# Three instead of two gate/up chunks by seven block products in three feed-forward layers, with plain chunks split between the halves of the features

## The chip, the cores and the metric

The kernel runs on one core of one Trainium2 chip. The metric is device time in microseconds (us) of one execution; the median of three runs stands for the kernel.

## The reference

A two-layer model on 256 tokens of 1024 features. Each layer is a half-weighted feed-forward block, a mixer (two kinds of attention) and another half-weighted feed-forward block; a norm closes the model. The change touches the feed-forward blocks alone:

```
D_MODEL, SEQ, DEPTH, D_FF = 1024, 256, 2, 2816

def swiglu(x, w_gate, w_up, w_down):
    return (jax.nn.silu(x @ w_gate) * (x @ w_up)) @ w_down

    for l in range(DEPTH):
        x = x + 0.5 * swiglu(rms_norm(x, ffa_norm[l]), ffa_w_gate[l], ffa_w_up[l], ffa_w_down[l])
        x = x + hybrid_mixer(rms_norm(x, mix_norm[l]), w_in[l], ...)
        x = x + 0.5 * swiglu(rms_norm(x, ffb_norm[l]), ffb_w_gate[l], ffb_w_up[l], ffb_w_down[l])
    return rms_norm(x, final_norm)
```

So there are four feed-forward blocks, called layers 0 to 3 here. All arrays are fp32.

## The kernel before

**Arithmetic.** Every fp32 matrix is split into a high and a low part (ScalarE copies the high part, L302 `whi`; VectorE subtracts it, L281 `wlo`), and every product is three matmuls of 128 x 512: high by high, low by high, high by low (`prod3`, L321 to L323).

**Weights.** The unit is a block of 512 rows by 512 columns (1 MB). `loader` brings blocks from HBM into five `raw` slots through SyncE's queue (L247, L238). `splitter` takes them in the order of the plan and splits each in two halves of 128 x 1024 into a pool of six `whi`/`wlo` pairs, so that three units are split ahead at most. TensorE frees a pair when it has used it.

**Gate and up.** The 2816 features are five chunks of 512 (0 to 4) and a rest `h5` of 256. A *plain* chunk c is `gc` and `uc`: the gate and the up weights, each two units (`kh`, the halves of the rows), each unit 24 matmuls. The other form takes a chunk's 2 x 2 block product (token halves by feature halves against gate and up) in *seven* block products instead of eight, with sums of blocks on both sides; each is one unit of 12 matmuls. The plan writes them as two digits: `53` is product 5 of chunk 3. The sums of activation blocks are made once for a layer (L515 to L530). The sums of weight blocks are made by DMA: an *add* of the next block onto the raw slot whose contents have just been split (`adder`, GpSimd's queue, L261, `accum_op=OP.add`). So products 1, 5, 6, 4 are a chain in one raw slot (three adds, the last with a gate block), 3 and 7 a chain in a second (one add), and 2 is a plain load. A slot in a chain is free again only after the last split of the chain. What leaves PSUM of such a chunk goes through `rest`, seven VectorE operations (L629 to L654) and two turns (transposes by TensorE, L549, and `hlo`, L556); a plain chunk has two VectorE operations (L574) and two turns.

**Order.** The program is written by a recorder with a clock of its own (class `Flow`); each engine then executes its instructions strictly in the written order, and waits for semaphores. The plan sets the order of the products on TensorE and of the splits:

```
PLANS = ("g0 u0 g2 11 u2 51 21 31 13 61 71 g4 41 53 23 33 u4 63 73 h5 43".split(),) + (
    "g0 u0 11 g2 51 21 31 u2 61 71 13 g4 41 53 23 33 u4 63 73 h5 43".split(),) * 3
```

The first plan is layer 0's, the second that of layers 1, 2 and 3. After gate and up comes the down product (11 units of 24 matmuls).

Of the kernel before, what the change touches and what calls it, by code (L numbers as in the profile page):

```python
# [41 lines left out]
ARRIVE_X = [3.5, 5.9, 8.1, 10.3]  # L42
HOP = 0.3
PLANS = ("g0 u0 g2 11 u2 51 21 31 13 61 71 g4 41 53 23 33 u4 63 73 h5 43".split(),) + (
    "g0 u0 11 g2 51 21 31 u2 61 71 13 g4 41 53 23 33 u4 63 73 h5 43".split(),) * 3
AC = 0.1
DV = 0.06

# [84 lines left out]
def hybrid_kernel(ctx, tc, x_in, ffa_norm, ffa_w_gate, ffa_w_up, ffa_w_down, mix_norm, w_in,  # L133
# [85 lines left out]
    def order(src, a, b, loads=1, **k):  # L219
        return Unit(Raw(src, a, b, loads), fine=loads > 1, **k)  # L220
# [95 lines left out]
    def cols(w, c0, n, kh):  # L316
        return w[kh * 512:(kh + 1) * 512, c0:c0 + n].rearrange("(k p) n -> p k n", p=128)
# [126 lines left out]
    def ffn_units(wg, wu, wd, plan, first):  # L444

        us = {}
        chain = {}

        def block(c, m, kh):
            return cols((wg, wu)[m], c * 512, 512, kh)

        def step(key, c, p, m, kh, end):

            src = block(c, m, kh)
            if key not in chain:
                chain[key] = (Raw(src, 4, 512), None)
                r = chain[key][0]
            else:  # L460
                r = Sum(chain[key][0], src, chain[key][1])
            us[p, c] = Unit(r, done=end)
            chain[key] = (chain[key][0], us[p, c])

        for z in plan:
            kind, c = z[0], int(z[1:])
            if kind in "gu":
                m = "gu".index(kind)
                for kh in range(2):
                    us[z, kh] = order(block(c, m, kh), 4, 512, loads=4 if first and z == plan[0] else 1)  # L470
            elif kind == "h":
                for kh in range(2):
                    us[z, kh] = order([cols(wg, 2560, 256, kh), cols(wu, 2560, 256, kh)], 4, 512)
            elif kind in "1564":
                step(("x", c), c, kind, *{"1": (0, 0), "5": (1, 0), "6": (1, 1), "4": (0, 1)}[kind], kind == "4")
            elif kind in "37":
                step(("y", c), c, kind, *{"3": (1, 1), "7": (1, 0)}[kind], z == [q for q in plan if q[0] in "37" and q[1:] == z[1:]][-1])
            else:
                step(("z", c), c, kind, 0, 1, True)
        for j in range(11):  # L480
            src = wd[j * 256:(j + 1) * 256].rearrange("(i p) n -> p i n", i=2)
            us["d", j] = order(src, 2, 1024)
        return us

    def ffn(us, nm, nxt, plan, last=False):
        hs = (big.tile([128, 22, 256], F32R, name="hhi", tag="hhi"),
              big.tile([128, 22, 256], F32R, name="hlo", tag="hlo"))
        rs = [nm.rs[:, t:t + 1] for t in range(T)]
        neg = small.tile([128, T], F32, name="neg", tag="neg", bufs=2)
        ev = {(c, t): Event() for c in range(6) for t in range(T)}  # L490
        sgs, forms, evs = {}, {}, {}
        inner = [i for i, z in enumerate(plan) if z[0] in "1234567"]

        def event(*k):
# [1135 lines left out]
```

## Time and profile before

| what | before |
|---|---|
| median of 3 runs | 1004.54 us (1003.06 to 1004.55) |
| the profiled execution's own time | 1003.62 us |
| its span, first to last instruction | 1001.8 us |
| TensorE / VectorE / ScalarE busy | 99% / 73% / 61% |
| gate/up stage of layers 1, 2, 3 (span's clock) | 321.7 to 441.2, 502.8 to 622.4, 813.4 to 933.0 us |

The span leaves out 1.8 us of the profiled execution's time. A stage is counted from the first matmul with the layer's normed input to the first with the gated features (`hhi`).

### The profile page before, as it was taken

How to read it: one execution, taken by the hardware profiler on the slowest of the kernel's cores; microseconds unless marked ns; L12 is line 12 of the kernel's file. 1: busy time of each engine (PE TensorE's matmuls, PEld its weight loads, DVE VectorE, ACT ScalarE, POOL GpSimd, SP SyncE). 2: the span in 40 equal slices, each digit the busy share in tenths (PEclk: the TensorE clock that was granted, in tenths of full speed). 3: DMA queues.
4: the chain of work that ended last, by engine and by line, in shares of the span. 5: the costliest groups of instructions: out<-in, count | busy, mean ns of one | idle time of the engine just before them, and what ended most of it. 6: DMA issues, size and time to landing. Idle time of an engine off the chain costs nothing.

```text
span 1001.8 us, 14198 instructions
## 1 busy us (share of the span) xinstructions
PE 988.3 (99%) x5270; PEld 825.7 (82%) x5270; DVE 735.8 (73%) x1369; ACT 608.0 (61%) x1055; POOL 53.5 (5%) x61
## 2 busy tenths in 40 slices
PE   8999999999999999999999999999999999999996
PEld 7888788898987888888888888888988878888885
DVE  6988764688887978784498768447878789788544
ACT  7667453558786676653367565336687766675531
POOL 1021000100000011100001110001000001110000
PEclk9999999999999999999999999999999999999999
DMA  9899965363743799965558998553655248999611
GB/s 334 273 198 303 290 241 183 106 193 119 260 145 103 208 248 278 274 251 200 179 151 229 300 262 274 196 166 116 211 188 191 86 130 226 281 264 305 237 48 42
DMA packets 100981, 207.62 MB, mean 207 GB/s; under 512 B 3784, under 2 KB 23376, under 8 KB 100912
## 3 DMA queue, kind: packets, MB, share of 16 engines
q1 hardware_dynamic: 83072, 171.65, 49.2%
q0 software_dynamic: 17536, 34.54, 19.3%
q8 instruction: 41, 0.67, 0.3%
q10 hardware_dynamic: 304, 0.53, 0.1%
q14 instruction: 28, 0.23, 0.1%
HBM read 205.66 MB, written 1.05 MB: 206 GB/s over the span
## 4 chain that ended last, share of the span: by engine, by line
PE 86%; DMA 4%; DVE 2%; ACT 1%; issue 1%; DVEq 0%; POOL 0%; ACTq 0%
PE acc L321 17%; PE acc L322 17%; PE acc L323 17%; PE sb L323 6%; PE sb L321 6%; PE sb L322 6%; PE acc L338 2%; DMA raw<-in_ffa_w_up_dram 2%; PE acc L339 2%; PE acc L340 2%; PE acc L1079 2%; PE tb L1059 2%; DMA raw<-in_ffa_w_gate_dram 2%; PE tb L549 2%; PE tb L407 1%; DVE wlo L281 1%
## 5 line engine op out<-in xcount | busy, mean ns | idle before, releaser
L281 DVE TENSOR_TENSOR wlo<-raw,whi 128x1024 fp32r<-128x1024 f32 (+2 forms) x404 | 450.2, 1136 | 166.7 <-ACT whi L302 166.3
L302 ACT ACTIVATE whi<-raw 128x1024 fp32r<-128x1024 f32 (+2 forms) x404 | 388.7, 990 | 239.7 <-PE acc L323 103.8
L321 PE MATMUL acc<-whi,hhi 128*128 128x512 f32 x352 | 138.4, 393 | 0.0
L323 PE MATMUL acc<-whi,hlo 128*128 128x512 f32 x352 | 137.2, 390 | 0.0
L322 PE MATMUL acc<-wlo,hhi 128*128 128x512 f32 x352 | 137.0, 389 | 0.0
L321 PE MATMUL acc<-whi,xhi 128*128 128x512 f32 (+1 forms) x336 | 131.9, 393 | 0.0
L322 PE MATMUL acc<-wlo,xhi 128*128 128x512 f32 (+1 forms) x336 | 128.1, 381 | 0.0
L323 PE MATMUL acc<-whi,xlo 128*128 128x512 f32 (+1 forms) x336 | 127.9, 381 | 0.0
L321 PE MATMUL sb<-whi,xhi 128*128 128x512 f32 x304 | 119.3, 392 | 0.0
L322 PE MATMUL sb<-wlo,xhi 128*128 128x512 f32 x304 | 118.4, 390 | 0.6 <-DVE wlo L281 0.6
L323 PE MATMUL sb<-whi,xlo 128*128 128x512 f32 x304 | 118.5, 390 | 0.0
L323 PEld LDWEIGHTS acc<-whi,hlo 128*128 128x128 f32 x352 | 66.1, 188 | 14.0
L322 PEld LDWEIGHTS acc<-wlo,hhi 128*128 128x128 f32 x352 | 66.1, 188 | 13.3
L321 PEld LDWEIGHTS acc<-whi,hhi 128*128 128x128 f32 x352 | 66.1, 188 | 13.4
L323 PEld LDWEIGHTS acc<-whi,xlo 128*128 128x128 f32 x336 | 63.1, 188 | 12.1
L321 PEld LDWEIGHTS acc<-whi,xhi 128*128 128x128 f32 x336 | 63.4, 189 | 11.2 <-issue 0.7
L322 PEld LDWEIGHTS acc<-wlo,xhi 128*128 128x128 f32 x336 | 63.2, 188 | 10.7 <-DVE wlo L281 0.2
L322 PEld LDWEIGHTS sb<-wlo,xhi 128*128 128x128 f32 x304 | 57.1, 188 | 12.6 <-DVE wlo L281 1.0
L323 PEld LDWEIGHTS sb<-whi,xlo 128*128 128x128 f32 x304 | 57.1, 188 | 12.0
L321 PEld LDWEIGHTS sb<-whi,xhi 128*128 128x128 f32 x304 | 57.1, 188 | 11.5
L338 PE MATMUL acc<-xhi,whi 128*128 128x256 f32 x192 | 56.5, 294 | 0.0
L340 PE MATMUL acc<-xhi,wlo 128*128 128x256 f32 x192 | 54.2, 282 | 0.0
(221 smaller groups left out, 1426.6 us busy)
## 6 DMA issues: line engine op xcount, KB each, us to landing
raw<-in_ffa_w_down_dram SPq DMA_DIRECT2D x22, 1024.0 KB, 5.0
raw<-in_ffb_w_down_dram SPq DMA_DIRECT2D x22, 1024.0 KB, 5.1
raw<-in_w_in_dram SPq DMA_DIRECT2D x20, 1024.0 KB, 5.1
raw<-in_ffb_w_gate_dram SPq DMA_DIRECT2D x20, 1024.0 KB, 5.2
raw<-in_ffa_w_gate_dram SPq DMA_DIRECT2D x18, 1024.0 KB, 7.4
raw<-in_ffa_w_up_dram SPq DMA_DIRECT2D x16, 1024.0 KB, 7.5
raw<-in_ffb_w_up_dram SPq DMA_DIRECT2D x16, 1024.0 KB, 6.4
raw<-in_ffa_w_up_dram POOLq DMA_DIRECT2D x12, 1024.0 KB, 9.3
```

Of the source, the lines that this page charges most:

```text
L281: nc.vector.tensor_tensor(view(u, lo, i, True), source(u, i), view(u, hi.bitcast(F32), i, True), OP.subtract)
L302: nc.scalar.activation(view(u, u.halves[-1][0], i, True), source(u, i), AF.Copy)
L321: nc.tensor.matmul(ps, xh, wh, start=first, stop=False, skip_group_check=True)
L322: nc.tensor.matmul(ps, xh, wl, start=False, stop=False, skip_group_check=True)
L323: nc.tensor.matmul(ps, xl, wh, start=False, stop=last, skip_group_check=True)
L338: nc.tensor.matmul(ps, wh, xs[0][:, k], start=first and j == 0, stop=False, skip_group_check=True)
L339: nc.tensor.matmul(ps, wh, xs[1][:, k], start=False, stop=False, skip_group_check=True)
L340: nc.tensor.matmul(ps, wl, xs[0][:, k], start=False, stop=last, skip_group_check=True)
L407: nc.tensor.transpose(ps[:, i * n + (t - ts[0]) * 128:i * n + (t - ts[0] + 1) * 128], x[:, t, k * 128:(k + 1) * 128], ident)
L549: nc.tensor.transpose(ps[:, j * 128:(j + 1) * 128], h[:, j * 128:(j + 1) * 128], ident)
L1059: nc.tensor.transpose(ps[:, j * 128:(j + 1) * 128], pp[:, i * n + s_ * 128:i * n + (s_ + 1) * 128], ident)
L1079: nc.tensor.matmul(grp.o[u * 64:(u + 1) * 64, h // 2 * 128:(h // 2 + 1) * 128], val(s_), pT[:, j * 128:(j + 1) * 128], start=u not in grp. ...
```

## The change

Layer 0 keeps its plan. In layers 1 to 3 chunk 2 too goes by seven products, chunk 4 stays plain and moves to the front, and of `u4` and `h5` the two units (`a`, `b`) may stand at different places of the plan; their PSUM sums wait in `parts` between the two.

```
-    "g0 u0 11 g2 51 21 31 u2 61 71 13 g4 41 53 23 33 u4 63 73 h5 43".split(),) * 3
+    "g0 u0 11 g4 51 21 12 31 22 61 u4a 52 u4b 13 32 71 41 62 23 53 72 h5a 33 42 63 h5b 73 43".split(),) * 3
...
-            kind, c = z[0], int(z[1:])
+            kind, c = z[0], int(z[1])
...
-                for kh in range(2):
-                    us[z, kh] = order(block(c, m, kh), 4, 512, loads=4 if first and z == plan[0] else 1)
+                for kh in rows_of(z):
+                    us[z[:2], kh] = order(block(c, m, kh), 4, 512, loads=4 if first and z == plan[0] else 1)
...
+    def rows_of(z):
+
+        return {"": (0, 1), "a": (0,), "b": (1,)}[z[2:]]
...
         def plain(z, tag, first):
-            c, then = int(z[1:]), {"g": gate, "u": up, "h": both}[z[0]]
-            ps = {}
-            for kh in range(2):
-                u = us[z, kh]
+            c, then = int(z[1]), {"g": gate, "u": up, "h": both}[z[0]]
+            ps = parts.setdefault(z[:2], {})
+            for kh in rows_of(z):
+                u = us[z[:2], kh]
```

Lines below L486 stand four lower in the changed kernel (L574 becomes L578, L549 becomes L553).

**VectorE, the long run.** Of before, layer 1, the splits of `41 53 23 33` (raw_3201 is chunk 1's chain, raw_3630 and raw_3862 are chunk 3's, raw_3770 is `23`), which are followed by the plain `u4`:

```order
L281 TENSOR_TENSOR wlo_3877<-raw_3201,whi_3876 128x1024
L281 TENSOR_TENSOR wlo_3892<-raw_3201,whi_3891 128x1024
L556 TENSOR_TENSOR hlo_3315<-tb_3885,hhi_3314 128x4x128
L281 TENSOR_TENSOR wlo_3905<-raw_3630,whi_3904 128x1024
L281 TENSOR_TENSOR wlo_3916<-raw_3630,whi_3915 128x1024
L281 TENSOR_TENSOR wlo_3934<-raw_3770,whi_3933 128x1024
L281 TENSOR_TENSOR wlo_3953<-raw_3770,whi_3952 128x1024
L649 TENSOR_TENSOR p_3563<-acc_3821,p_3563 128x512
L281 TENSOR_TENSOR wlo_3968<-raw_3862,whi_3967 128x1024
L281 TENSOR_TENSOR wlo_3980<-raw_3862,whi_3979 128x1024
L654 SCALAR_TENSOR_TENSOR p_3666<-p_3666,neg_3316,p_3563 128x512
```

Of the change, layer 1, from the end of `u4b` on: `32` (raw_3814), `71` (raw_3515), `41` (raw_3201), in which the two L578 take `u4`'s results out of PSUM.

```order
L578 SCALAR_TENSOR_TENSOR sg_3639<-sb_3780,rs_3234,sg_3639 128x512
L281 TENSOR_TENSOR wlo_3859<-raw_3814,whi_3858 128x1024
L578 SCALAR_TENSOR_TENSOR sg_3648<-sb_3790,rs_3234,sg_3648 128x512
L281 TENSOR_TENSOR wlo_3870<-raw_3814,whi_3869 128x1024
L560 TENSOR_TENSOR hlo_3315<-tb_3880,hhi_3314 128x4x128
L281 TENSOR_TENSOR wlo_3887<-raw_3515,whi_3886 128x1024
L560 TENSOR_TENSOR hlo_3315<-tb_3896,hhi_3314 128x4x128
L281 TENSOR_TENSOR wlo_3904<-raw_3515,whi_3903 128x1024
L281 TENSOR_TENSOR wlo_3922<-raw_3201,whi_3921 128x1024
L281 TENSOR_TENSOR wlo_3938<-raw_3201,whi_3937 128x1024
L638 TENSOR_TENSOR p_3666<-acc_3927,p_3666 128x512
L643 TENSOR_TENSOR z_3951<-acc_3644,p_3563 128x512
```

Before, four units in a row (with three other operations in the rows shown) are followed by a plain chunk; now `13 32 71 41 62 23 53 72` are eight in a row, and what three chunks and `u4` leave in PSUM stands between them.

**VectorE, the second part of that run.** Of before, behind the run, `u4` (raw_3898, raw_3921), `63` (raw_3630) and `73` (raw_3862):

```order
L281 TENSOR_TENSOR wlo_3997<-raw_3898,whi_3996 128x1024
L281 TENSOR_TENSOR wlo_4010<-raw_3898,whi_4009 128x1024
L556 TENSOR_TENSOR hlo_3315<-tb_4015,hhi_3314 128x4x128
L281 TENSOR_TENSOR wlo_4027<-raw_3921,whi_4026 128x1024
L281 TENSOR_TENSOR wlo_4040<-raw_3921,whi_4039 128x1024
L281 TENSOR_TENSOR wlo_4057<-raw_3630,whi_4056 128x1024
L281 TENSOR_TENSOR wlo_4068<-raw_3630,whi_4067 128x1024
L281 TENSOR_TENSOR wlo_4083<-raw_3862,whi_4082 128x1024
L281 TENSOR_TENSOR wlo_4094<-raw_3862,whi_4093 128x1024
```

Of the change: from the first split of `23` (raw_3934) over `53` (raw_3768) to the second of `72` (raw_3814). Three rows not shown (two splits of `62` and one L648) stand between the fence above and this one.

```order
L281 TENSOR_TENSOR wlo_3972<-raw_3934,whi_3971 128x1024
L653 TENSOR_TENSOR p_3563<-acc_3927,p_3563 128x512
L281 TENSOR_TENSOR wlo_3984<-raw_3934,whi_3983 128x1024
L560 TENSOR_TENSOR hlo_3315<-tb_3977,hhi_3314 128x4x128
L633 TENSOR_TENSOR p_3713<-p_3713,acc_3986 128x512
L635 TENSOR_TENSOR p_3839<-p_3839,p_3713 128x512
L281 TENSOR_TENSOR wlo_3998<-raw_3768,whi_3997 128x1024
L658 SCALAR_TENSOR_TENSOR p_3666<-p_3666,neg_3316,p_3563 128x512
L281 TENSOR_TENSOR wlo_4017<-raw_3768,whi_4016 128x1024
L281 TENSOR_TENSOR wlo_4031<-raw_3814,whi_4030 128x1024
L560 TENSOR_TENSOR hlo_3315<-tb_4039,hhi_3314 128x4x128
L281 TENSOR_TENSOR wlo_4051<-raw_3814,whi_4050 128x1024
```

Where the plain chunk's splits stood, with one other operation between them, are now the splits of three more products, with six.

**SyncE, the loads in the middle of the stage.** Of before, layer 1: `13`, `g4` (two), `23`, `33`, `u4` (two).

```order
L247 DMA raw_3630<-in_ffb_w_gate_dram 128x4x512
L247 DMA raw_3698<-in_ffb_w_gate_dram 128x4x512
L247 DMA raw_3722<-in_ffb_w_gate_dram 128x4x512
L247 DMA raw_3770<-in_ffb_w_gate_dram 128x4x512
L247 DMA raw_3862<-in_ffb_w_up_dram 128x4x512
L247 DMA raw_3898<-in_ffb_w_up_dram 128x4x512
L247 DMA raw_3921<-in_ffb_w_up_dram 128x4x512
```

Of the change: `u4a`, `u4b`, `13`, `32`, `23`, and `h5a` (two pieces).

```order
L247 DMA raw_3630<-in_ffb_w_up_dram 128x4x512
L247 DMA raw_3722<-in_ffb_w_up_dram 128x4x512
L247 DMA raw_3768<-in_ffb_w_gate_dram 128x4x512
L247 DMA raw_3814<-in_ffb_w_up_dram 128x4x512
L247 DMA raw_3934<-in_ffb_w_gate_dram 128x4x512
L238 DMA raw_3957<-in_ffb_w_gate_dram 128x4x256
L238 DMA raw_3957<-in_ffb_w_up_dram 128x4x256
```

After the load of `32` (raw_3814) all five slots hold chains (`x1` raw_3201, `y1` raw_3515, `x2` raw_3460, `x3` raw_3768, `y2` raw_3814); the load of `23` (raw_3934) takes the slot of raw_3515, which is free after the second split of `71`. Before, the load of `23` (raw_3770) takes the slot that `71` left one plain chunk earlier.

## Rows read from the trace of the kernel before

**Rows 1.** The page, parts 1 and 2: busy time, and 40 slices.

```profile
span 1001.8 us, 14198 instructions
PE 988.3 (99%) x5270; PEld 825.7 (82%) x5270; DVE 735.8 (73%) x1369; ACT 608.0 (61%) x1055; POOL 53.5 (5%) x61
...
PEclk9999999999999999999999999999999999999999
DMA  9899965363743799965558998553655248999611
```

**Rows 2.** Busy time by stretch: the gate/up stages of layers 1, 2, 3.

```profile
core 0: us, PE busy (x) PEld busy (x) DVE busy (x) ACT busy (x) POOL busy (x), PEclk, DMA share, GB/s
321.70:441.20 119.50, 119.36 (x547) 98.71 (x546) 98.24 (x123) 78.91 (x99) 10.29 (x8) 1.00 0.89 247
502.80:622.40 119.60, 119.60 (x551) 99.11 (x550) 98.41 (x123) 77.53 (x100) 10.26 (x8) 1.00 0.89 246
813.40:933.00 119.60, 119.46 (x547) 98.60 (x546) 97.97 (x122) 78.94 (x99) 11.43 (x10) 1.00 0.90 251
```

**Rows 3.** Timeline of TensorE, layer 3: start, us, line (12 matmuls lie between).

```profile
890.14 0.39 PE L321 MATMUL acc<-whi,xhi 128*128 128x512 f32 x1
...
891.50 0.39 PE L321 MATMUL acc<-whi,xhi 128*128 128x512 f32 x1
...
892.86 0.39 PE L321 MATMUL acc<-whi,fnhi 128*128 128x512 f32 x1
...
900.12 0.39 PE L321 MATMUL acc<-whi,fohi 128*128 128x512 f32 x1
```

**Rows 4.** The chain that ended last: one turn's four transposes.

```profile
389.84 0.44 PE tb L549 x4
```

**Rows 5.** VectorE's groups by form, layer 3's gate/up: busy, mean ns, idle before.

```profile
L281 DVE TENSOR_TENSOR wlo<-raw,whi 128x1024 fp32r<-128x1024 f32 x59 | 70.9, 1220 | 19.1 <-ACT whi L302 19.0
L556 DVE TENSOR_TENSOR hlo<-tb,hhi 128x512 fp32r<-128x512 f32 x9 | 6.2, 684 | 0.1
...
L574 DVE SCALAR_TENSOR_TENSOR sg<-sb,rs,sg 128x512 f32<-128x512 f32 x4 | 2.8, 740 | 0.0
...
L631 DVE TENSOR_TENSOR p<-p 128x512 f32<-128x512 f32 x2 | 1.4, 692 | 0.1
```

**Rows 6.** Timeline of VectorE, layer 3, in two stretches.

```profile
874.94 0.69 DVE L631 TENSOR_TENSOR p<-p 128x512 f32<-128x512 f32 x1
875.55 0.68 DVE L556 TENSOR_TENSOR hlo<-tb,hhi 128x512 fp32r<-128x512 f32 x1
...
879.61 0.74 DVE L644 SCALAR_TENSOR_TENSOR z<-z,neg,sg 128x512 f32<-128x512 f32 x1
880.27 3.49 DVE L281 TENSOR_TENSOR wlo<-raw,whi 128x1024 fp32r<-128x1024 f32 x3
...
893.67 2.35 DVE L281 TENSOR_TENSOR wlo<-raw,whi 128x1024 fp32r<-128x1024 f32 x2
```

**Rows 7.** ScalarE's groups by form in the same stage.

```profile
L302 ACT ACTIVATE whi<-raw 128x1024 fp32r<-128x1024 f32 x59 | 61.1, 1059 | 29.6 <-PE sb L323 12.2 <-DMA raw<-in_ffb_w_up_dram 9.4 <-PE acc L323 6.6
```

**Rows 8.** Busy time by stretch: loads alone, then adds alone.

```profile
841.00:844.00 3.00, 3.00 (x15) 2.49 (x14) 2.32 (x4) 2.73 (x5) 0.00 (x0) 1.00 1.05 403
850.00:853.00 3.00, 3.00 (x15) 2.49 (x14) 1.53 (x2) 3.00 (x4) 0.00 (x0) 1.00 1.13 208
```

**Rows 9.** DMA issues of five short windows, one load each (819, 848, 858, 868, 877 us): us to landing.

```profile
raw<-in_ffb_w_gate_dram SPq DMA_DIRECT2D x1, 1024.0 KB, 5.0
...
raw<-in_ffb_w_gate_dram SPq DMA_DIRECT2D x1, 1024.0 KB, 8.6
...
raw<-in_ffb_w_gate_dram SPq DMA_DIRECT2D x1, 1024.0 KB, 15.1
...
raw<-in_ffb_w_gate_dram SPq DMA_DIRECT2D x1, 1024.0 KB, 8.1
...
raw<-in_ffb_w_up_dram SPq DMA_DIRECT2D x1, 1024.0 KB, 7.4
```

**Rows 10.** DMA issues of three short windows, one add each (846, 853, 861 us): us to landing.

```profile
raw<-in_ffb_w_up_dram POOLq DMA_DIRECT2D x1, 1024.0 KB, 9.2
...
raw<-in_ffb_w_up_dram POOLq DMA_DIRECT2D x1, 1024.0 KB, 12.1
...
raw<-in_ffb_w_gate_dram POOLq DMA_DIRECT2D x1, 1024.0 KB, 12.9
```

More of the change, by code (lines that the diff above doesn't have):

```diff
@@ L465, in ffn_units @@
         for z in plan:
-            kind, c = z[0], int(z[1:])
+            kind, c = z[0], int(z[1])
             if kind in "gu":
                 m = "gu".index(kind)
-                for kh in range(2):
-                    us[z, kh] = order(block(c, m, kh), 4, 512, loads=4 if first and z == plan[0] else 1)
+                for kh in rows_of(z):
+                    us[z[:2], kh] = order(block(c, m, kh), 4, 512, loads=4 if first and z == plan[0] else 1)
             elif kind == "h":
-                for kh in range(2):
-                    us[z, kh] = order([cols(wg, 2560, 256, kh), cols(wu, 2560, 256, kh)], 4, 512)
+                for kh in rows_of(z):
+                    us[z[:2], kh] = order([cols(wg, 2560, 256, kh), cols(wu, 2560, 256, kh)], 4, 512)
             elif kind in "1564":
@@ L490, in ffn @@
         ev = {(c, t): Event() for c in range(6) for t in range(T)}
-        sgs, forms, evs = {}, {}, {}
+        sgs, forms, evs, parts = {}, {}, {}, {}
         inner = [i for i, z in enumerate(plan) if z[0] in "1234567"]
@@ L589, in plain @@
         def plain(z, tag, first):
-            c, then = int(z[1:]), {"g": gate, "u": up, "h": both}[z[0]]
-            ps = {}
-            for kh in range(2):
-                u = us[z, kh]
+            c, then = int(z[1]), {"g": gate, "u": up, "h": both}[z[0]]
+            ps = parts.setdefault(z[:2], {})
+            for kh in rows_of(z):
+                u = us[z[:2], kh]
                 order_ = [(t, i) for t in range(T) for i in range(4)] if first else [(t, i) for i in range(4) for t in range(T)]
```

## The prediction

> **What bounds the kernel now.** I read the page first: TensorE is busy for 99% of the span, at the full granted clock in all 40 slices, and no other engine is over 73% [rows 1]. An average over stages says nothing about one stage, so the second view is the busy time of the three stretches that the change touches: in each gate/up stage TensorE is busy for practically all of 119.5 us, VectorE for 98.2, ScalarE for 79, and the DMA engines have a share of 0.89 [rows 2]. So TensorE sets the end, but VectorE and the DMA engines stand close behind it there, far closer than their averages. The third view is what ended VectorE's idle time in that stage: 19.1 us, nearly all waits for ScalarE's `whi` [rows 5], and ScalarE's own waits before `whi` are for TensorE (12.2 and 6.6 us, a pair of the pool that is not yet used up) and for an add's landing (9.4 us) [rows 7]. The splits run ahead of TensorE and are held back by it: the second split of `41` ends at 883.76 and TensorE needs it at 891.50; four products later the second split of `33` ends at 896.02 and is needed at 900.12 [rows 3, 6]. The lead was 7.7 us and is 4.1 us: a run of products of the seven-product kind eats it, a plain chunk restores it. That is the place to look at.
>
> **What is removed.** A plain chunk is 96 matmuls, a seven-product chunk 84. Twelve matmuls take 2.72 us (890.14 to 892.86) [rows 3], so each layer loses 2.72 us of TensorE's work, three layers 8.16 us, and a stage without waits would take 119.5 - 2.7 = 116.8 us.
>
> **What is added, as totals.** Three units more for a layer are six splits, 6 x 1.22 = 7.3 us on VectorE [rows 5]; the way out of PSUM has seven operations instead of two, 5 x 0.69 = 3.5 us. VectorE then has 98.2 + 10.8 = 109 us of work in 116.8. ScalarE gets 6 x 1.06 = 6.4 us of copies [rows 7], two PSUM copies more at about half that each, and stays under 87. The adds go from 8 to 12, the plain loads of gate and up from 20 to 19. Loads alone move 403 GB/s and adds alone 208 [rows 8], so a 1 MB block (1.049 MB) is 2.6 us as a load and 5.0 us as an add: 8 x 5.0 + 20 x 2.6 = 92 us before, 12 x 5.0 + 19 x 2.6 = 109 us after. Both resources have work for 93% of the stage. As totals they still fit; the question is the order.
>
> **The early run, `51 21 12 31 22 61`.** Back to back a split takes (3.49 - 1.22) / 2 = 1.135 us [rows 6], so two splits are 2.27 us against 2.72 us of TensorE for each unit, and hardly anything else stands between these splits on VectorE (what leaves PSUM comes later). VectorE gains on TensorE. I cost it at nothing; the cover is that 0.45 us a unit.
>
> **The long run, `13 32 71 41 62 23 53 72`.** Let T be the end of `u4b` on TensorE. VectorE's queue has `u4`'s first result (L578) ahead of the split of `32`; it can't start before T. From this L578 to the second split of `72` stand 27 instructions: 14 splits, 4 of the scalar-tensor-tensor kind (L578 twice, L648, L658) and 9 others of 512 columns. Back to back the second kind takes 0.66 us (879.61 to 880.27) and the third 0.60 (874.94 to 875.55 gives 0.61) [rows 6]. The sum is 14 x 1.135 + 4 x 0.66 + 9 x 0.60 = 23.9 us. TensorE, without waits, gets to the second half of `72` after 7 products and a half, 7.5 x 2.72 = 20.4 us, and four turns at 0.44 [rows 4], 1.8 us: 22.2 us. So VectorE alone, without one idle moment, is 23.9 + 0.1 (its result's way) - 22.2 = **1.8 us** late at the end of the run. What was 19.1 us of idle time for the stage doesn't help, since this queue can't begin earlier.
>
> **The load of `23` in that run.** All five raw slots hold chains once `32` is loaded; the load of `23` waits for the second split of `71`. That is the eighth of the 27 instructions: 4 splits, 2 L578, 2 L560, 4.54 + 1.32 + 1.2 = 7.1 us, so it is issued at about T + 7.2. A load alone lands after 5.0 us; four loads that met adds landed after 7.4, 8.1, 8.6 and 15.1 us [rows 9]. After landing come a `whi` (1.06) and a `wlo` (1.22) with their hand-overs, 2.5 us. With 5.0 the split of `23` ends at T + 14.7, just when VectorE's queue reaches it anyway (15 instructions before it). Each microsecond more is idle time on VectorE, with everything behind it late. Is an add in flight there? GpSimd's queue issues the adds for `71`, `41`, `62`, `53`, `72` in this order. The first can go when `31` is split, about 4 us before TensorE uses it, and from there TensorE has `31`, `22`, `61`, `u4a`, `52`, `u4b`, 4 x 2.72 + 2 x 5.44 = 21.8 us, up to T: about T - 26. The last can go after the second split of `32`, the fourth of the 27 instructions, T + 3.7. Five adds are 25 us at 208 GB/s, and the loads of `u4b`, `13` and `32` in that time 8 us more: the 33 us from T - 26 to T + 7 are about full, and adds issued close to another landed after 12.1 and 12.9 us instead of 9.2 [rows 10]. So I don't take 5.0. Of the three usual values I take the shortest, 7.4, since the rest of this sum has no slack in it: the split of `23` is 2.4 us late, and with the 1.8 the long run costs **4.2 us**. Bounds: 1.8 (landing 5.0) and 5.4 (8.6).
>
> **The end, `63 h5b 73 43`.** The last add of the stage (for `43`) can be issued only after the second split of `63`, and this needs the pair that `h5a` frees. From there TensorE has `33`, `42`, `63`, `h5b`, `73` and two turns' worth of transposes, 4 x 2.72 + 5.44 + 0.9 = 17.2 us. The split of `63` takes 2.5 us of them, the add 9.2 to 12.9 [rows 10], the split of `43` 2.5: 14.2 to 17.9. So the wait is 0 to 0.7 us; I take 0, and keep 0.7 for the range. Splitting `h5` and `u4` itself costs TensorE nothing: the same 24 matmuls for each half.
>
> **Sum.** Each layer: -2.72 + 4.2 = +1.5 us; three layers +4.4 us. The profiled execution took 1003.62 us, so 1008.0 by this sum; the median of the runs stands 0.9 us higher, 1004.54, which gives 1009.0.
>
> **The rivals.**
> *The load of `23` comes in time.* If the adds ahead of it have drained by T + 7, it lands after 5 us and only VectorE's 1.8 us are left: -0.9 us a layer, -2.8 us, 1001.8. For it: before, no load of these blocks ever made TensorE wait in layers 1 to 3. Against it: those 33 us of adds and loads in the 33 us from T - 26 to T + 7. This ends on the other side of no change (faster); the point from which it decides is a landing under 5.9 us, where 1.8 + 0.9 eats the 2.72 exactly.
> *VectorE's backlog never shows.* The splits might carry enough lead into the run that TensorE doesn't notice, and the whole 8.16 us come back: 996.4. For it: VectorE has 7.8 us a stage to spare by the totals. Against it: L578 holds the queue at T. The Trainium skill's page Perfetto Trace Analysis (Identifying the Most-Contended Engine) takes the occupancy of VectorE as a fair measure of how close it is to its limit; by that rule 93% would leave it off the path and this rival would come true, while rows 5 and 6 show its lead shrink at 82%.
> *The adds' queue becomes the bound.* Twelve adds behind each other; if the load of `23` meets the 15.1 us of [rows 9], the run costs 1.8 + 10.1 = 11.9 us, +9.2 us for such a layer. Once among three: 9.2 + 2 x 1.5 = +12.2, 1016.7. For it: 109 us of DMA work in 116.8. Against it: that landing needed a second load just ahead, and SyncE has none there.
> *It cancels.* A landing of 5.3 to 6.6 us makes the run cost 2.1 to 3.4 us: within 2 us of no change.
>
> **Numbers.** Forecast (the run costs 3.4 to 5.4 us a layer): 0.48, its own range 1006.5 to 1012.5. Load in time: 0.17. No backlog: 0.10. Cancels: 0.15. Adds' queue: 0.10. A measurement of this kernel can tell 0.2%, 2 us, from no change. Faster 0.27, same 0.15, slower 0.58. The range leaves out the full saving below and half of the adds' queue above: 1000 to 1015.
>
> **What would show it.** In the stages of layers 1 to 3: 492 matmuls instead of 504 and twelve adds. The chain of waits should hold, once a layer, TensorE waiting for `wlo` in the products `23` to `72`, 3 to 5 us together, with VectorE there waiting for `whi` and ScalarE for a load of the gate weights of 7 us or more; and none before `u4b`. If TensorE waits there but ScalarE never for that load, VectorE's queue alone is the cause; if TensorE waits for a `wlo` of `43`, it is the adds. The prediction is wrong if these stages take 117 us, or if the waits come in the early run.

## The result, and the profile after

The changed kernel takes 1063.95 us, median of 4 runs (1063.40 to 1064.61), against 1004.39 for the kernel before (4 runs): a ratio of 1.0596, 95% interval 1.0583 to 1.0610. I had forecast 1009.0, range 1000 to 1015: the sign was right, the size far off. The profiled execution took 1064.30 us.

The page of the changed kernel, parts 1 and 2, answers [rows 1]:

```profile
span 1062.5 us, 14210 instructions
PE 1001.3 (94%) x5234; PEld 826.8 (78%) x5234; DVE 763.0 (72%) x1402; ACT 624.6 (59%) x1079; POOL 68.9 (6%) x73
...
PEclk9999999999999998899999998999999999998999
```

TensorE has 36 matmuls less to do, and yet is busy 13 us longer and idle about 48 us longer; in three places its granted clock dips. Busy time by stretch, the three gate/up stages, answers [rows 2]:

```profile
core 0: us, PE busy (x) PEld busy (x) DVE busy (x) ACT busy (x) POOL busy (x), PEclk, DMA share, GB/s
321.86:463.25 141.39, 123.80 (x533) 99.29 (x532) 105.00 (x131) 84.36 (x107) 15.42 (x12) 0.94 0.89 223
525.05:665.04 139.99, 123.28 (x538) 98.80 (x536) 104.95 (x133) 82.59 (x108) 15.42 (x12) 0.96 0.89 225
856.17:993.81 137.64, 123.81 (x533) 99.08 (x532) 105.00 (x131) 84.36 (x107) 16.55 (x14) 0.95 0.91 233
```

21.9, 20.4 and 18.0 us more than before: together 60.3 us, practically the whole loss. One row is worth a second look beside [rows 2]: share times stretch is the DMA engines' work, 0.89 x 119.5 = 106 us before and 0.89 x 141.4 = 126 us now. What TensorE waited for in layer 1's stage (us in total, times, longest):

```profile
PE tb L553 <- DVE p L658: 7.5, 1, 7.5
PE tb L553 <- DVE sg L578: 4.6, 2, 4.3
PE acc L322 <- DVE wlo L281: 2.2, 2, 1.4
PE acc L321 <- DVE p L638: 2.0, 2, 1.1
PE acc L321 <- ACT whi L302: 1.1, 1, 1.1
```

The two long ones are turns, not products. The next views show what is behind them. First GpSimd's queue in that stage, start of each issue; the five rows are the adds for `61`, `52`, `71`, `41`, `62`:

```profile
354.93 1.28 POOL L261 DMA_DIRECT2D raw<-in_ffb_w_up_dram  x1 [13.17 <-DVE wlo L281]
361.79 1.27 POOL L261 DMA_DIRECT2D raw<-in_ffb_w_up_dram  x1 [5.58 <-DVE wlo L281]
365.00 1.27 POOL L261 DMA_DIRECT2D raw<-in_ffb_w_up_dram  x1 [1.93 <-DVE wlo L281]
370.44 1.28 POOL L261 DMA_DIRECT2D raw<-in_ffb_w_gate_dram  x1 [4.17 <-DVE wlo L281]
375.79 1.27 POOL L261 DMA_DIRECT2D raw<-in_ffb_w_up_dram  x1 [4.07 <-DVE wlo L281]
```

Five adds in 21 us; before, consecutive adds of layer 1 stood 7.0 us apart at the least. Then what became of them and of the loads beside them: DMA issues of eight short windows of layer 1, us to landing, in order the add of `71` (365 us), the load of `u4b` (367), the add of `41`, the load of `13` (372), the add of `62`, the load of `32` (384), the load of `23` (404) and the add of `73` (431):

```profile
raw<-in_ffb_w_up_dram POOLq DMA_DIRECT2D x1, 1024.0 KB, 15.0
...
raw<-in_ffb_w_up_dram SPq DMA_DIRECT2D x1, 1024.0 KB, 13.2
...
raw<-in_ffb_w_gate_dram POOLq DMA_DIRECT2D x1, 1024.0 KB, 17.9
...
raw<-in_ffb_w_gate_dram SPq DMA_DIRECT2D x1, 1024.0 KB, 16.5
...
raw<-in_ffb_w_up_dram POOLq DMA_DIRECT2D x1, 1024.0 KB, 20.3
...
raw<-in_ffb_w_up_dram SPq DMA_DIRECT2D x1, 1024.0 KB, 12.5
...
raw<-in_ffb_w_gate_dram SPq DMA_DIRECT2D x1, 1024.0 KB, 8.1
...
raw<-in_ffb_w_up_dram POOLq DMA_DIRECT2D x1, 1024.0 KB, 15.3
```

The load of `23`, the only one that I had priced (7.4 us), is near its price. `u4b`, `13` and `32`, which I had taken as on time, need 12.5 to 16.5 us, the adds 15 to 20 instead of 9 to 13 [rows 10]. Busy time by stretch from 365 to 395 us in layer 1, three rows of the change and then the same three of before:

```profile
365.00:375.00 10.00, 10.00 (x46) 8.29 (x45) 8.56 (x8) 8.34 (x10) 2.55 (x2) 1.00 1.12 235
375.00:385.00 10.00, 10.00 (x46) 8.28 (x45) 4.23 (x5) 2.01 (x2) 1.27 (x1) 1.00 1.10 262
385.00:395.00 10.00, 7.82 (x34) 5.50 (x33) 3.02 (x3) 2.49 (x3) 1.29 (x1) 1.00 1.05 257
...
365.00:375.00 10.00, 10.00 (x46) 8.29 (x45) 5.50 (x6) 5.16 (x6) 1.27 (x1) 1.00 1.09 292
375.00:385.00 10.00, 10.00 (x50) 8.38 (x49) 9.10 (x12) 6.74 (x8) 1.28 (x1) 1.00 1.09 272
385.00:395.00 10.00, 10.00 (x48) 8.26 (x47) 9.70 (x11) 5.60 (x7) 0.00 (x0) 1.00 1.07 311
```

The DMA share, last but one, is 1.05 to 1.12, and [rows 8] has 1.05 and 1.13 for loads and adds that fill the engines: they are full. But they are about as full before (1.07 to 1.09), where TensorE is busy all the time. So a full stretch alone is not the loss; what differs is how soon TensorE needs the blocks. An estimate with the prediction's 2.72 us for a product, 5.0 for an add and 2.6 for a load: the run `13 32 71 41 62 23 53 72` takes TensorE 22 us, and its five adds and three loads are 33 us of DMA work. Before, `13 g4 41 53 23 33 u4` took TensorE 35 us, and its two adds and seven loads were 28.

How adds and loads share the engines shows in the packets of one microsecond (383.5 to 384.5 us; q0 is the queue of the adds, q1 that of the loads; packets, MB, share):

```profile
q0 software_dynamic: 64, 0.13, 70.4%
q1 hardware_dynamic: 64, 0.13, 39.2%
```

From 372 to 393 us each queue moves about 64 packets and 0.13 MB a us, where adds alone moved 0.21 and loads alone 0.40 [rows 8]. So a 1 MB block, of either kind, is under way for 8 us: the adds of `71`, `41` and `62` land at 380.0, 388.3 and 396.1 us, the loads of `u4b`, `13` and `32` at 380.2, 388.9 and 396.3.

Last, how one late block becomes a wait of TensorE: the timelines of ScalarE, VectorE and TensorE around `h5b` in layer 1, and the granted clock behind it (busy time by stretch, PEclk third from the right):

```profile
446.19 1.06 ACT L302 ACTIVATE whi<-raw 128x1024 fp32r<-128x1024 f32 x1 [10.15 <-DMA raw<-in_ffb_w_up_dram]
447.15 0.71 ACT L543 ACTIVATE p<-p,rs 128x512 f32<-128x512 f32 x1
...
448.42 0.74 DVE L658 SCALAR_TENSOR_TENSOR p<-p,neg 128x512 f32<-128x512 f32 x1
...
449.31 1.09 PE L553 MATMUL tb<-ident,p 128*128 128x128 f32 x4 [7.53 <-DVE p L658]
...
445.10:455.30 10.20, 5.99 (x17) 4.90 (x18) 6.14 (x7) 4.27 (x5) 0.00 (x0) 0.50 0.81 199
```

ScalarE stands 10.15 us at the copy of `73`, whose add lands only at 446.1 us; behind it in its queue is the gate of chunk 2's second tile (L543), which VectorE's L658 needs, which TensorE's turn in the middle of `h5b` needs. TensorE is idle for 7.5 us there, and the granted clock stands at half (0.50, 1.2 of 2.4 GHz) up to 455.3.

### The profile page after: what moved, and what is told of

The parts are those of the page before. It is cut to its first block, busy times and chain, and to the rows that moved or that the text cites. A ratio compares the mean times of both kernels' runs of the same rounds, so it can differ in the third digit from the quotient of the medians.

```text
span 1062.5 us, 14210 instructions
## 1 busy us (share of the span) xinstructions
PE 1001.3 (94%) x5234; PEld 826.8 (78%) x5234; DVE 763.0 (72%) x1402; ACT 624.6 (59%) x1079; POOL 68.9 (6%) x73
## 3 DMA queue, kind: packets, MB, share of 16 engines
HBM read 215.09 MB, written 1.05 MB: 203 GB/s over the span
## 4 chain that ended last, share of the span: by engine, by line
PE 61%; DMA 19%; DVE 8%; issue 3%; ACT 3%; DVEq 0%; ACTq 0%; POOL 0%; SPq 0%; POOLq 0%
PE acc L321 13%; PE acc L322 13%; PE acc L323 13%; DMA raw<-in_ffb_w_up_dram 8%; DMA raw<-in_ffa_w_up_dram 7%; DVE wlo L281 5%; DMA raw<-in_ffa_w_gate_dram 2%; PE acc L338 2%; PE acc L339 2%; PE acc L340 2%; ACT whi L302 2%; PE acc L1083 2%; PE sb L321 2%; PE sb L322 2%; PE tb L1063 2%
## 5 line engine op out<-in xcount | busy, mean ns | idle before, releaser
L281 DVE TENSOR_TENSOR wlo<-raw,whi 128x1024 fp32r<-128x1024 f32 (+2 forms) x422 | 470.7, 1139 | 202.9 <-ACT whi L302 201.7
L302 ACT ACTIVATE whi<-raw 128x1024 fp32r<-128x1024 f32 (+2 forms) x422 | 403.6, 992 | 289.4 <-PE acc L323 102.4
L321 PE MATMUL acc<-whi,xhi 128*128 128x512 f32 (+1 forms) x372 | 147.0, 395 | 8.7 <-DVE p L638 6.0
L322 PE MATMUL acc<-wlo,xhi 128*128 128x512 f32 (+1 forms) x372 | 143.5, 386 | 3.1 <-DVE wlo L281 2.9
L323 PE MATMUL acc<-whi,hlo 128*128 128x512 f32 x352 | 137.2, 390 | 0.0
L321 PE MATMUL sb<-whi,xhi 128*128 128x512 f32 x208 | 84.4, 406 | 0.0
L322 PEld LDWEIGHTS acc<-wlo,xhi 128*128 128x128 f32 x372 | 70.4, 189 | 17.9 <-DVE wlo L281 6.2
L322 PE MATMUL sb<-wlo,xhi 128*128 128x512 f32 x208 | 83.4, 401 | 0.8 <-DVE wlo L281 0.8
L323 PE MATMUL sb<-whi,xlo 128*128 128x512 f32 x208 | 82.9, 399 | 0.0
L339 PE MATMUL acc<-xlo,whi 128*128 128x256 f32 x192 | 54.2, 282 | 0.0
L261 POOL DMA_DIRECT2D raw<-in_ffb_w_up_dram x18 | 23.1, 1285 | 414.4 <-DVE wlo L281 414.4
L322 PEld LDWEIGHTS sb<-wlo,xhi 128*128 128x128 f32 x208 | 40.5, 195 | 9.8 <-DVE wlo L281 1.6
```

What stands on the lines that cost most here:

```text
L261: nc.gpsimd.dma_start(r.tile[:, :r.a * r.b].rearrange("p (a b) -> p a b", a=r.a), z.src, accum_op=OP.add)
L281: nc.vector.tensor_tensor(view(u, lo, i, True), source(u, i), view(u, hi.bitcast(F32), i, True), OP.subtract)
L302: nc.scalar.activation(view(u, u.halves[-1][0], i, True), source(u, i), AF.Copy)
L321: nc.tensor.matmul(ps, xh, wh, start=first, stop=False, skip_group_check=True)
L322: nc.tensor.matmul(ps, xh, wl, start=False, stop=False, skip_group_check=True)
L323: nc.tensor.matmul(ps, xl, wh, start=False, stop=last, skip_group_check=True)
```

## The experiments

Three theories. **Adds:** the adds' transfers and the loads among them ask more of the DMA engines in two stretches than these carry, and blocks land late. **Order:** late blocks would do little, but the written order puts results that TensorE needs at once behind them (the picture just shown). **Clock:** half the clock after each wait is a good part of the loss. All three layers have the same stage, so most runs put a different edit into each layer; the unchanged change has 141.4, 140.0 and 137.6 us there, so that a few us between layers say nothing. The stages below are from the profiles.

**1. Take the adds away.** A dictionary for each layer says how a product's block comes: as an add, as a plain load without the sum, or not at all (the first entry is layer 0, which stays).

```
-            nc.gpsimd.dma_start(r.tile[:, :r.a * r.b].rearrange("p (a b) -> p a b", a=r.a), z.src, accum_op=OP.add)
+            dst = r.tile[:, :r.a * r.b].rearrange("p (a b) -> p a b", a=r.a)
+            if z.how == "add":
+                nc.gpsimd.dma_start(dst, z.src, accum_op=OP.add)
+            elif z.how == "load":
+                nc.gpsimd.dma_start(dst, z.src)
+OUT = [{}, {'all': 'none'}, {'all': 'load'}, {'71': 'none', '41': 'none', '62': 'none'}]
```

> Plan of the change in all three layers; only how the twelve adds of a layer move data differs. Layer 1: no add is issued at all. Layer 2: each add is a plain load of the same block, without the sum (half an add's time by rows 8). Layer 3: the adds of products 71, 41 and 62 alone are left out. The sums that these adds make are left out of the result; the instructions of the four engines stay in the same order. Stages after the change: 141.4, 140.0 and 137.6 us; before: 119.6. Adds' queue (the loads of u4b, 13, 32 and of what follows share the DMA engines with adds that wait for each other): layer 1 near 117 to 119, layer 2 under 122, layer 3 loses most of the waits of the run 13 to 72 and keeps those at the end, 125 to 132. VectorE's queue (27 instructions of 23.9 us from u4's first L578 on, and the L658 behind a split in h5b): the order is unchanged, so layer 1 keeps a good part of the loss, 125 or more.

Measured, busy time by stretch:

```profile
322.75:442.58 119.83, 117.46 (x533) 95.91 (x532) 104.83 (x131) 85.16 (x107) 0.00 (x0) 1.00 0.48 158
504.39:624.90 120.51, 117.94 (x538) 96.24 (x536) 104.84 (x132) 83.40 (x108) 9.04 (x12) 1.00 0.77 262
816.06:945.85 129.79, 119.96 (x533) 97.02 (x532) 104.71 (x132) 84.74 (x107) 12.71 (x11) 0.97 0.83 223
```

Without adds 119.8 us, with plain loads in their place 120.5: the adds are the whole loss against before, with every instruction of the four engines in its place. DMA work falls from 126 to 58 us, so an add is 68 / 12 = 5.7 us of it and, as a load, (0.77 x 120.5 - 57.5) / 12 = 2.9. The 125 or more that was expected if VectorE's queue and the order are the cause did not come. But 119.8 is also not the 116.8 that I had for a stage without waits. The same in all three layers, timed:

> The change with all adds of layers 1 to 3 left out (their sums are missing from the result), timed. If adds are all of the loss beyond the 3 us a layer of waits that the run without adds still had, the time is that of before within 0.2%: 1003.5 to 1006.5. If the three layers act on each other (a slower stage shifts what the next one finds loaded), it lies outside.

1004.80 us against 1003.63: 1.0013, interval 1.0004 to 1.0023. The change with free adds is no gain either. TensorE's waits in layer 1's stage:

```profile
PE acc L329 <- DVE p L647: 2.0, 2, 1.1
PE acc L330 <- DVE wlo L289: 0.2, 1, 0.2
```

L647 (L638 of the change) reads the bank of a 7 before the 4 of the same chunk may add to it. Before, a plain chunk stood between `71` and `41`; now they are neighbours, twice in a layer counting `73 43`, and TensorE waits 1 us each time. VectorE's backlog hardly shows (0.2).

**2. Where.** The same edit, other products.

```
+OUT = [{}, {'73': 'none', '43': 'none'}, {'71': 'none', '41': 'none', '62': 'none', '73': 'none', '43': 'none'}, {'41': 'none', '62': 'none'}]
```

> The same plan, adds left out by place (with their sums). Layer 1: the adds of 73 and 43, at the end. Layer 2: those of 71, 41, 62, 73 and 43. Layer 3: those of 41 and 62. Adds' queue: layer 1 loses the 12 us gap before the second half of h5b, 141.4 to about 130; layer 2 loses both places, 117 to 121; layer 3 frees 10 us of DMA ahead of the loads of 13 and 32, 137.6 to about 126 to 132. VectorE's queue: leaving adds out moves nothing in its order, all three lose less than 5 us.

130.1, 122.8 and 131.2 us: without the two adds at the end 11.3 less, without five 17.2 less, without `41` and `62` 6.4 less; `71`, `41` and `62` gave 7.8 above. So the end is worth more than the run (by different layers), and both together nearly all. In layer 2 what I had priced, the load of `23` among the adds of `53` and `72`, is left: this load took 8.3 us there, and TensorE's waits were

```profile
PE acc L330 <- DVE wlo L289: 2.1, 2, 1.4
PE acc L329 <- DVE p L647: 2.0, 2, 1.1
```

**3. How much of the adds.** Cut each to part of its rows, or leave out one chunk's four.

```
+OUT = [{}, {'all': '2'}, {'all': '3'}, {'all': '1'}]
...
+                n = int(z.how)
+                nc.gpsimd.dma_start(dst[:, :n], z.src[:, :n], accum_op=OP.add)
```

> The change with every add cut to a part of its block (the rest of each sum left out): layer 1 two of four rows, 0.5 MB; layer 2 three of four, 0.75 MB; layer 3 one of four, 0.25 MB. Twelve adds at 5.7 us of DMA work each (share times span: 125 us with all, 57 without) make 57 + 34 = 91, 57 + 51 = 108 and 57 + 17 = 74 us of DMA work. By the adds' queue the loss sets in only when little is spare: layer 3 119.5 to 120.5, layer 1 120 to 123, layer 2 124 to 132, the change itself 137 to 141. If the wait is for the fixed part of an add's way (2 us to its first packet) and not for its bytes, the three stand close together, all above 125.

119.9, 130.2 and 119.9 us with shares of 0.79, 0.84 and 0.66: adds cut to half cost nothing, adds cut to three quarters half of the loss. The number of adds and the fixed part of their way don't matter; their bytes do.

```
+OUT = [{}, {'51': 'none', '61': 'none', '71': 'none', '41': 'none'}, {'52': 'none', '62': 'none', '72': 'none', '42': 'none'}, {'53': 'none', '63': 'none', '73': 'none', '43': 'none'}]
```

> The change with eight adds a layer instead of twelve, as many as before: the four adds of one chunk are left out (with their sums), of chunk 1 in layer 1, of chunk 2 in layer 2, of chunk 3 in layer 3. The DMA engines' work falls from 125 to about 103 us, under the 106 us with which the kernel before has no wait. If only the total counts, all three stages are at 119.8 to 121. If it is how closely adds follow each other ahead of what needs them, the stages that keep the pair 73, 43 (layers 1 and 2) keep its loss, 126 to 131, and layer 3, which keeps 71, 41, 62 close together and loses the pair at the end, 125 to 130.

131.7, 129.0 and 132.1 us. With eight adds, a total of 0.78 x 131.7 = 103 us, under the 106 of before, each stage still loses 9 to 12 us. In layer 1, where the add of `73` is issued at 422.2 us, among the loads of the first blocks of the down projection, and lands after 14.6 us, one wait is most of it:

```profile
PE tb L562 <- DVE p L667: 7.1, 1, 7.1
PE acc L330 <- DVE wlo L289: 2.0, 2, 1.4
PE acc L329 <- DVE p L647: 2.0, 2, 1.1
```

So not the total of the stage decides, but what meets in a stretch.

**4. The order.** First the scheduler's price of an add, which moves instructions only.

```
+ADD = {0: (3.1, 2.0), 1: (5.0, 2.0), 2: (6.9, 2.0), 3: (6.9, 5.0)}
...
-            loader.last = max(fl.clock + 2.0, loader.last) + 3.1
+            loader.last = max(fl.clock + 2.0, loader.last) + z.cost[0]
```

> The change with another cost of an add in the scheduler's model, which decides nothing but the order in which each engine's instructions are written: 5.0 us (layer 1), 6.9 (layer 2) and 6.9 with a landing 5 us later (layer 3), in place of 3.1 with 2.0. All transfers and all work stay. The two longest waits of the change are turns: TensorE waits for a result (L578, L658) that VectorE has behind the split of a block that has not landed (12.1 of the 17.4 us of waits in layer 1). If the order is what turns late adds into such a loss, a truer cost puts these results ahead of the late splits and the stages fall to 125 to 132; if the DMA engines' work is the floor, they stay within 5 us of 141.4, 140.0, 137.6, and TensorE waits for wlo in place of the turns.

136.3, 147.2 and 150.9 us: 5 better, 7 and 13 worse. In layer 1 the turns wait for 3.2 us together instead of 12.1, and `whi` and `wlo` take over (6.8 us instead of 3.3). To move nothing else, the split of one block was held behind one result:

```
+                if u.hold is not None:
+                    yield u.hold
                 yield u.raw.landed[i + u.step - 1]
...
+            if c == 2 and "73" in held:
+                us["7", 3].hold.set(fl.clock)
```

> The change, all transfers and all work as they are; only VectorE's order (and ScalarE's copy that belongs to it) moves by one split. Layer 1: the split of 73 stands behind L658, on which TensorE's turn inside h5b waits (7.5 us), in place of ahead of it. Layer 2: the first split of 32 stands behind u4's second L578, on which the other turn waits. Layer 3: both. If what turns the late adds into loss is that a result stands behind a split whose block has not landed, the stages fall by what those turns wait: layer 1 by 6 to 10 us (141.4 to 131 to 135), layer 2 by 3 to 6, layer 3 by 8 to 14. If the late block is the loss itself, TensorE only waits a product later, for wlo of 73 and of 32, and each stage falls by under 3 us.

139.8, 140.2 and 141.3 us: -1.6, +0.2, +3.7. Layer 1's waits now:

```profile
PE tb L560 <- DVE sg L597: 3.9, 1, 3.9
PE acc L324 <- ACT whi L305: 3.2, 2, 1.6
PE acc L325 <- DVE wlo L282: 3.1, 4, 1.4
PE tb L560 <- DVE sg L585: 2.3, 1, 2.3
PE acc L324 <- DVE p L647: 1.8, 2, 1.0
```

The 7.5 us at L658 are gone, and most of it has come back: for `whi` and `wlo` of late blocks and, 3.9 us, for a result of `h5` (L597), which VectorE now has behind the split of `43`, whose add has not landed:

```profile
453.17 1.23 DVE L282 TENSOR_TENSOR wlo<-raw,whi 128x1024 fp32r<-128x1024 f32 x1 [2.68 <-ACT whi L305]
454.31 0.48 DVE L597 SCALAR_TENSOR_TENSOR sg<-sb,rs,sg 128x256 f32<-128x256 f32 x1
```

That is the same pattern one place further, so this run doesn't say what a better order could give. A bound stands in the unchanged change, layer 1: the first split of `43`, and TensorE's start of `43`:

```profile
452.99 1.23 DVE L281 TENSOR_TENSOR wlo<-raw,whi 128x1024 fp32r<-128x1024 f32 x1 [0.76 <-ACT whi L302]
...
460.43 0.47 PE L321 MATMUL acc<-whi,xhi 128*128 128x512 f32 x1 [1.14 <-DVE p L638]
```

With this landing of its add, `43` could not start before the split ends, at 454.2 us; it started at 460.4. So in layer 1 a better order could give back at most 6.2 of the 21.9 us (the price of 5.0 us gave 5.1); for the rest the last block itself is late. The order is a part of the loss, and not its cause.

**5. The clock.**

```
+FILL = [{}, {2: 24}, {4: 16}, {2: 24, 4: 16}]
...
+            for _ in range(fill.get(c, 0) if t == 1 else 0):
+                nc.tensor.matmul(ps, nm.xs[0][:, 0, :128], nm.xs[0][:, 0:2].rearrange("p a b -> p (a b)"), start=True, stop=True)
```

> The change with idle work for TensorE, whose result nothing reads, ahead of a transposition that waits for VectorE: in layer 1 24 matmuls of 512 columns (5.4 us) in the turn of chunk 2's second token tile (L658), in layer 2 16 of them (3.6 us) in that of chunk 4 (L578), in layer 3 both. If the half clock behind each wait is a good part of the loss, the stretches at half clock behind these two places get shorter and the stages fall by up to half of what ran at half clock there: layer 1 by 3 to 5 us (141.4 to 137), layer 2 by 1 to 3, layer 3 by 3 to 6. If the clock only follows the waits and costs little, the stages stay within 1 us, since the idle work fits into the wait; if the filled wait is shorter than the work, they rise by what doesn't fit.

138.3, 139.6 and 139.7 us at 0.98 to 0.99 of the clock instead of 0.94 to 0.96: -3.1, -0.4, +2.1. Layer 1 falls as the clock's theory expected, layers 2 and 3 miss it; together that is -1.4 of 60.3 us, with the slow stretches nearly gone. TensorE is busy 6.3 us longer in the change's layer 1 than in the run without adds (123.8 against 117.5); about half of that came back there, and in the other two layers next to nothing did.

**6. Other plans.**

```
+         "g0 u0 11 g4 51 21 12 31 22 61 u4 52 13 32 71 41 62 23 53 72 h5 33 42 63 73 43".split(),
+         "g0 u0 11 g2 51 21 31 u2 61 71 13 g4 41 53 23 33 u4a 63 u4b 73 h5a 43 h5b".split(),
+         "g0 u0 11 51 21 31 61 71 41 g4 12 52 22 32 u4 62 72 42 13 53 23 33 h5 63 73 43".split())
```

> Another plan in each layer, all sums made. Layer 1: three chunks by seven products as in the change, but u4 and h5 whole: 12 adds of 1 MB stay in nearly the same order, so by the adds' queue it stays slow (132 to 145), by the splitting of the halves as the cause it falls to 117 to 122. Layer 2: two chunks by seven products as before, u4 and h5 split in their halves: by the adds' queue (8 adds) 119 to 122, by the splitting as the cause 125 or more. Layer 3: three chunks one behind the other in place of interleaved, 51 21 31 61 71 41, then 12 52 22 32 62 72 42, then 13 53 23 33 63 73 43: each add stands close behind the split that it waits for, so TensorE should wait for adds more often than in the change (145 or more) if what counts is the time from issue to need, and less if what counts is adds queued behind each other.

135.5, 124.2 and 164.1 us. Whole `u4` and `h5` don't cure it. Split halves aren't free by themselves either: with two chunks they cost 4.6 us, one wait of a turn for a result of a split half (2.9) and 1.8 us that TensorE is busy longer; that is 2 us above what was expected for the adds as the cause. Chains one behind the other are worst, as expected if the time from issue to need counts.

```
-    "g0 u0 11 g4 51 21 12 31 22 61 u4a 52 u4b 13 32 71 41 62 23 53 72 h5a 33 42 63 h5b 73 43".split(),) * 3
...
+         "g0 u0 11 g4 51 21 12 31 22 61 u4a 52 u4b 13 32 71 62 41 23 53 72 h5a 33 42 63 73 h5b 43".split(),
...
+OUT = [{}, {'all': 'none'}, {'all': 'load'}, {}]
```

> The plan of the change with two pairs of neighbours taken apart: 71 62 41 in place of 71 41 62, and 63 73 h5b 43 in place of 63 h5b 73 43, so that no product 4 stands right behind the 7 whose bank it adds to. Layer 1: no add is issued (sums left out); layer 2: adds as plain loads (sums left out); layer 3: adds as they are. If without adds the change is still no gain (119.8 in the run that left all adds out) because TensorE waits twice for the VectorE operation that reads the bank of a 7 before the 4 behind it may add to it (2.0 us), layer 1 falls to 117.0 to 118.3 and layer 2 to 117.5 to 119; if VectorE's backlog of 1.8 us is what is left, both stay at 119.5 to 120.5. Layer 3: by the adds' queue 133 to 142 as in the change (137.6), since the same adds are issued at nearly the same times.

124.2 without adds, 126.0 with loads in their place and 137.2 us with the adds: the first two a miss, the third as expected. The waits behind a 7 are gone, but the new order brings one of 3.0 us for L652 (which reads the bank of a 3) and one of 2.0 for a `wlo`, without any add. Two more orders without adds, and a sum made by GpSimd in place of the DMA engines:

```
+            elif z.how == "pool":
+                nc.gpsimd.tensor_tensor(r.tile, r.tile, r.tile, OP.add)
+         "g0 u0 11 g4 51 21 12 31 22 61 u4a 52 13 32 71 u4b 41 62 23 53 72 h5a 33 42 63 73 h5b 43".split(),
+         "g0 u0 11 g4 51 21 12 31 22 61 u4a 52 u4b 13 32 71 41 62 23 53 72 h5a 33 42 63 73 h5b 43".split())
```

> What is left without the adds' transfers. Layer 1: the plan of the change; in place of each add GpSimd adds the 1 MB tile to itself once the split before it is done (the second block is not loaded: its load and the right sum are left out). If GpSimd's sum is no dearer than an add (4 us or so for 2048 columns, against 8.9 us to landing) and disturbs VectorE little, the stage stays at 119.8 to 121; if the two slow each other down, 125 or more. Layers 2 and 3: no adds at all (sums left out) with two other orders: 71 u4b 41 with 73 h5b 43, and 71 41 with 73 h5b 43. If TensorE's wait behind a 7 costs about 1 us a time, layer 3 is 1.0 us under the 119.8 of the change without adds, layer 2 1.5 to 2.5 under it; if orders make new waits of 3 us as the pair 62 41 did (124.2), both are 120 or more.

147.8, 125.4 and 120.0 us. No order without adds came under 119.8. And GpSimd's sums cost more than the adds: in layer 1 VectorE's splits (mean ns of one, second number) and GpSimd's sums were

```profile
L289 DVE TENSOR_TENSOR wlo<-raw,whi 128x1024 fp32r<-128x1024 f32 x62 | 101.4, 1666 | 4.4 <-ACT whi L310 4.3
...
L269 POOL TENSOR_TENSOR raw<-raw 128x2048 f32<-128x2048 f32 x12 | 54.9, 4572 | 202.2 <-DVE wlo L289 196.1 <-DMA raw<-in_ffb_w_up_dram 6.1
```

Last, adds in halves, each half issued as soon as its part of the block before is split:

```
+            for i in range(2):
+                yield z.before.ready[2 * i + 1]
...
+                nc.gpsimd.dma_start(dst[:, 2 * i:2 * i + 2], z.src[:, 2 * i:2 * i + 2], accum_op=OP.add)
```

> Each add issued as two transfers of 0.5 MB, the first as soon as the first half of the block before it in its chain is split. Layer 1: plan of the change; layer 2: plan with 71 62 41 and 73 h5b 43; layer 3: plan of before with its two seven-product chunks. Bytes are the same. If the time from issue to landing counts (8.9 us for an add that meets nothing, 13 to 20 us in the queue), each add starts 1 to 1.5 us earlier and its first half can be split 3 us earlier: layers 1 and 2 fall by 5 to 12 us. If the DMA engines' total is the bound, they fall by less than 4. Layer 3: 119.6 as before (TensorE never waits there), or 120 to 122 if twice as many transfers cost DMA time.

137.1, 130.4 and 119.5 us. The change's order gains 4.3, a little under what was expected; the order that was 137.2 with whole adds (in another layer) gains 6.8; before's plan gains nothing. Three more orders with these halves:

> All sums made, each add as two transfers of 0.5 MB, three orders: layer 1 71 u4b 41 and 73 h5b 43; layer 2 71 41 and 73 h5b 43; layer 3 u4 and h5 whole with 71 62 41 and 73 43. With the change's order this gave 137.1, with 71 62 41 and 73 h5b 43 130.4. By the DMA engines' work (124 us of share times span in both) no order gets under 124; I expect 128 to 138. An order under 119.5 would beat the kernel before; by the spacing of adds alone (no cap by their sum) it could be there.

139.5, 130.9 and 131.9 us. None of the seven orders of three chunks that ran with all their adds came under 130; before has 119.6.

## Why the prediction was wrong

**The step that failed** is in the part on the long run: "Is an add in flight there?" was asked for the load of `23` alone, and the loads of `u4b`, `13` and `32` and the adds for `71`, `41` and `62` were left on time. I had counted the very transfers, five adds of 25 us and loads of 8 us in 33 us, and called that stretch "about full", then drew no price for the blocks that lay in it. By my own count this work was done at T + 7, but TensorE needs `32` one product after T; its load landed at 396.3 us, 7 us after T. Leaving out `71`, `41`, `62` gave back 7.8 us. The same step failed at the end of the stage, where it cost more (below).

**The totals** were a little too kind. I summed the DMA work by rates to 92 us before and 109 after, as time of full engines. Share times stretch gives 106 before ([rows 2]) and 126 after, but it counts full engines as 1.05 (loads) to 1.13 (adds) [rows 8]. In that measure my counts make 8 x 5.0 x 1.13 + 20 x 2.6 x 1.05 = 100 and, after, 120: 6 us short both times. So an estimated 115 us of full engines, not 109, had to fit into 116.8, and in the first 18 us of layer 1's stage the share is 0.47. But eight adds at 103 us lose 9 to 12 us as well: the total was a warning, what meets in a stretch decides.

**The long run, 4.2 us.** The mechanism that I priced exists: 2.1 us with the late adds out, within its bounds of 1.8 to 5.4, and the load of `23` took 8.1 us in the change. It is a tenth of the loss. *VectorE's 1.8 us:* not there; with free adds 0.2 to 0.3 us. The Trainium skill's rule (Perfetto Trace Analysis, Identifying the Most-Contended Engine), which I had let stand for the rival without a backlog, takes VectorE's occupancy as a measure of its limit; here it agrees with the trace without adds, 104.8 of 119.8 us busy and off the path. The saving that this rival promised did not come even so (1004.80 us).

**The end, 0 to 0.7 us.** The largest miss: 11.3 us by the run without the adds of `73` and `43`. I took 9.2 to 12.9 us for an add and looked only at `43`. The add of `73`, issued among the loads of `h5b` and of the first three blocks of the down projection, took 15.3, and that of `43` 15.9. From 437 to 446 us the trace has about 50 packets of each queue in a us, 0.10 MB of the adds beside 0.20 MB of the down projection's loads, whose packets are twice as large: the add moves at half of its speed.

**What I didn't price at all:** 2.0 us a layer behind `71` and `73`, since a 4 adds to the bank that VectorE reads after the 7. With it and 0.9 us that TensorE was busy beyond the 116.6 of its own work (119.33 - 2.72), the gain of 2.72 is eaten without any add.

**What was right:** the sign, but by luck: with the 2.1 us measured for the one term that was there, the sum is -2.72 + 2.1 = -0.6 us a layer, no slower than before; what made it slower was not in the sum. Rightly foreseen were no wait in the early run, nor before 386 us in layer 1, and 105 of VectorE's 109 us. The rival of the adds' queue was the mechanism, with 0.10 and 9.2 us in one layer of three, at one load; it was about 20 in each. What I said would show it, a wait for a `wlo` of `43`, did not come: the adds showed as waits of two turns for results whose own blocks had long landed.

**How `71`, `41` and `62` came late** can be read from the landings: each landed about 8 us behind the add before it (371.9 for `52`, then 380.0, 388.3, 396.1); an estimated 5.0 of these 8 are its own by [rows 8], 3 come from the loads beside it. Of the 15.0, 17.9 and 20.3 us from issue to landing, 6.9, 9.6 and 12.5 were waits for the add ahead.

**Open:** what the best order of three chunks would reach with all its adds. No run removes the waits for late blocks and keeps all the adds' bytes, and the landings move with the order.

## What to carry to other kernels

Price a transfer by what is in flight with it. For each stretch of the plan, set the DMA work of its blocks beside TensorE's time for the same products, and where it is more (33 against 22 us here), take every block in it as late, also those that were always on time. That the engines are full says less: before, they were as full there, and nothing waited. Check a sum made from rates against the busy share that the profile shows for the same stage before using it for the change, and in the same measure. And where an accumulating product follows the one whose bank must be read first, count that wait: a reordering that makes neighbours of them cost it each time here (about 1 us).

## What the runs showed of the hardware

- An add cost the DMA engines 5.7 us of work for 1 MB, the same block as a load 2.9 (share times stretch, in which full engines showed 1.05 to 1.13).
- While adds and loads were under way together (372 to 393 us of layer 1), each queue moved about 64 packets a us. With packets of equal size that was 0.13 MB each, against 0.21 for adds and 0.40 for loads alone; beside the down projection's loads, with packets twice as large, it was 0.10 against 0.20.
- With GpSimd adding 1 MB tiles (4.57 us each), VectorE's splits went from 1219 to 1666 ns, its busy time in the stage from 105 to 138 us. The Trainium skill (SBUF — State Buffer, Who interferes with whom) says that a VectorE instruction with two inputs in SBUF contends with a GpSimd instruction that reads SBUF; the split has two, and the run agrees.
- After waits of 4.3 and 7.5 us TensorE's granted clock stood at half, after waits of 1.1 us (without adds) it stayed at 1.00. Keeping TensorE busy through the waits kept the clock at 0.98 to 0.99 and changed the three stages by -3.1, -0.4 and +2.1 us.
